# Forgetting attention in a two-layer trunk: layer 1's projections run four steps ahead, its keys move as 80 partitions, and the row of maxima is made by transposes

## The chip, the cores and the metric

The kernel runs on one core of one Trainium2 chip. The metric is the time of the program on the device in microseconds (us), as the median of several runs.

## The reference, cut to what matters

One sequence of 2048 rows of 1024 channels goes through two layers. Layer 0 is a gated recurrence beside a pooling mixer; the change does not touch it. Layer 1 is attention with a forget bias, 16 heads of 64 channels:

```python
def odd_mixer(h, w_in, b_f, qnorm_g, knorm_g, w_out):
    proj = (h @ w_in).astype(jnp.float32)
    q, k, v, g, fl = jnp.split(proj, [FOX_WIDTH, 2 * FOX_WIDTH, 3 * FOX_WIDTH, 4 * FOX_WIDTH], axis=-1)
...
    q = rms_norm(hd(q), qnorm_g).transpose(0, 2, 1, 3)
    k = rms_norm(hd(k), knorm_g).transpose(0, 2, 1, 3)
...
    logf = jax.nn.log_sigmoid(fl + b_f.astype(jnp.float32))
    cumf = jnp.cumsum(logf, axis=1).transpose(0, 2, 1)
...
        logits = (jnp.einsum('bhqd,bhkd->bhqk', q[:, :, q0:q1], k[:, :, :q1]) * scale
                  + cumf[:, :, q0:q1, None] - cumf[:, :, None, :q1])
        mask = jnp.arange(q0, q1)[:, None] >= jnp.arange(q1)[None, :]
        probs = jax.nn.softmax(jnp.where(mask, logits, -jnp.inf), axis=-1)
        outs.append(jnp.einsum('bhqk,bhkd->bhqd', probs, v[:, :, :q1]))
    o = jnp.concatenate(outs, axis=2).transpose(0, 2, 1, 3).reshape(b_, s_, FOX_WIDTH)
    o = o * jax.nn.silu(g)
    return o.astype(h.dtype) @ w_out
```

The term of the query's own `cumf` cancels in the softmax, so that the kernel adds to each logit only the key's bias and takes away the query's maximum.

## The kernel before, in words

**Segments.** The 2048 rows are taken as four segments of 512 (`s` = 0 to 3). For each, layer 0 runs and then layer 1; the output projection of layer 1 of a segment is woven into layer 0 of the next. Float32 numbers are split in a high and a low part (`split_lo`, L182), and a projection makes three matmul passes over the parts: one step of it (`proj_N`, or one step of a gate) is 8 x 3 matmuls of 128x256 (or 128x512 for the gates) on TensorE.

**Keys and queries of a head.** `prep(s, h)` (L1057) makes four transposes `pqkT` out of the normalised projection `qk`, and from them `Q1`, `K1` (128 partitions: high and low parts) and `Q3`, `K2` (68 partitions: 64 channels and 4 rows of constants and biases). The rows 64 to 67 of `K2` come by a transfer from `cfd` (high and low part of the key's bias, 1, 1; L1078), those of `Q3` from `q4d` (1, 1, 0, 0; L1077). `K1` and `K2` are also stored in DRAM, as `k1d` and `k2d`, for the later segments, which load them again as `K1o` (128 x 512) and `K2o` (68 x 512; `old_k2`, three buffers).

**Maximum.** `max_pass(s, h)` multiplies `Q3` by all keys (`pmx`), reduces each product along the keys on VectorE (L1100, L1102) to `m` (L1107: 128 queries x 4 blocks), makes `-m` and its low part (`mh` L1110, `mhl` L1111 and L1112), transposes `mhl` in one matmul (`pmt`), copies it to `mr` (L1117), and a transfer on ScalarE's queue (L1118) writes the rows 66 and 67 of `Q3`.

**Attention of a head.** `attend(s, h)` goes over blocks of 128 keys: `pst` is `K1` by `Q1` plus `K2` by `Q3` (68 rows: key channels, the bias, minus the maximum), plus a mask `mk` in the diagonal blocks. ScalarE takes the exponential twice (`ph` L1157, `pst` L1158), VectorE makes the low part `pl` (L182), GpSimd adds the sum `la`, and TensorE multiplies by the values (`pov`, `pol`). At the end, ScalarE copies a half of the result (`u`, L1179) and splits `la` (`lh`, L1184). The first product with `Q3` of a head is the first instruction that needs its maxima.

**Order.** `quad_attention` interleaves `attend` of head h with `max_pass` of head h+1; at the end of head h it runs `prep(h+2)`. Into this, `weave` puts the steps of `fill` on TensorE, evenly: `quad_fill(s, j)` is the queries and keys of two pairs of heads (`qk_pair`, 4 steps each), the gates of a quad of heads (4 steps) and the values of the next quad (`v_quad`, 4 steps), 16 steps in all, 8 for the last quad. Before each quad of heads, `fill` is made anew, and it is drained at its end; `need` drains it up to the pair that `prep` reads. `fill` of quad 0 is there from before head 0, and `keep=16` keeps all 16 steps of it for the quad. The last quad's fill also takes the first steps of the next segment (`pre0`). A scheduler then sets each engine's queue, by program order as a priority; an engine takes its instructions in order. Weights are loaded on SyncE's queue (`raw`, L288), cast on ScalarE (`wt`, L293), and their low part is made by VectorE or GpSimd (L182).

**Normalisation.** `qk_pair` copies each product (L1015), squares it (L1017), sums (L1018), takes a reciprocal root on 16 numbers a row (`rsqrt_mean`, L164 to L172) and multiplies (L1022) before the pair's first transposes.

All matmuls stand in the profile under L40 and all transposes under L43, the lines of the two helpers; in the changed file those are L42 and L45.

Of the kernel before, what the change touches and what calls it, by code (L numbers as in the profile page):

```python
# [27 lines left out]
VW = 2 * HD + 2  # L28
EPS = 1e-6
# [4 lines left out]
def trunk(ctx, tc, x, cvec, norm_g, ada_c, ada_w, ada_b, ada_bg, lbp, w0, w0o, w1, w1f, w1o,  # L34
# [118 lines left out]
    k2d = dr.tile([NH, HD + 4, T], F32, name="k2d")  # L153
    vd = dr.tile([NH, P, T // P, VW], F32, name="vd")
    cfd = dr.tile([NH, 4, T], F32, name="cfd")
    q4d = dr.tile([4, SEG], F32, name="q4d")
# [819 lines left out]
    def forget_rows(s, act):  # L976
# [22 lines left out]
        nc.sync.dma_start(cfd[:, 0, s * SEG:(s + 1) * SEG], f(ch_))  # L999
        nc.sync.dma_start(cfd[:, 1, s * SEG:(s + 1) * SEG], f(cl))  # L1000
# [56 lines left out]
    def prep(s, h):  # L1057
# [19 lines left out]
        nc.scalar.dma_start(f(Q3[HD:HD + 4]), q4d)  # L1077
        nc.scalar.dma_start(f(K2[HD:HD + 4]), cfd[h, :, s * SEG:(s + 1) * SEG])  # L1078
        if s < NSEG - 1:
            nc.sync.dma_start(k1d[h, :, s * SEG:(s + 1) * SEG], f(K1))  # L1080
            nc.sync.dma_start(k2d[h, :, s * SEG:(s + 1) * SEG], f(K2[0:HD + 4]))
        L["ops", h] = (Q1, Q3, K1, K2)

    def old_k2(h, c):
        K2 = kp.tile([P, SEG], F32R, name="K2o", tag="k2o", bufs=3)
        nc.sync.dma_start(f(K2[0:HD + 4]), k2d[h, :, c * SEG:(c + 1) * SEG])
        return K2

    def max_pass(s, h):
# [30 lines left out]
    def attend(s, h):  # L1120
# [18 lines left out]
        for c in range(s + 1):  # L1139
# [8 lines left out]
            for b in range(NTB):  # L1148
# [4 lines left out]
                mm(st[:, q0:], k2[0:HD + 4, ks], Q3[0:HD + 4, q0:], start=False, stop=(c < s))  # L1153
# [54 lines left out]
    LAG = 2  # L1208

# [23 lines left out]
    def layer1(s, xs):  # L1233
# [155 lines left out]
```

## Time and profile before

| | us |
|---|---|
| median of 3 runs | 3073.19 (3065.78 to 3075.12) |
| the profiled execution | 3059.16 |
| its span in the profile | 3057.4 |
| TensorE busy | 2799.8 (92%) |
| VectorE busy | 2373.8 (78%) |
| ScalarE busy | 1792.8 (59%) |
| GpSimd busy | 1191.7 (39%) |

The span goes from the first to the last instruction. Busy times of the engines overlap. PE is TensorE, DVE VectorE, ACT ScalarE, POOL GpSimd and SP SyncE; names of tiles stand without buffer numbers, so `Q<-mr` is the transfer of L1118 (`Q` is Q3), `K` and `Q` stand for K1, K2, Q1, Q3. [...]

### The profile page before, as it was taken

To read this page: it belongs to the slowest core of one execution; us is meant where nothing else is said; L and a number is where in the kernel's file an instruction comes from. 1 tells how busy PE (TensorE), PEld (TensorE's weight loads), DVE (VectorE), ACT (ScalarE), POOL (GpSimd) and SP (SyncE) were. 2 spreads that over 40 slices of the span, in tenths; PEclk is the share of its full clock that TensorE was granted. 3 is DMA by queue.
4 is the path that set the end of the run, shared out by engine and by line. 5 is a ranking of instruction groups with operands and counts; after the bars stand their busy time and mean duration, and the time that the engine had idled before them with its cause. 6 is when DMAs were issued, how large, how long until landed. Compare 5 with 4: busy or idle time off the path is not lost.

```text
span 3057.4 us, 49147 instructions
## 1 busy us (share of the span) xinstructions
PE 2799.8 (92%) x17020; PEld 2378.7 (78%) x17020; DVE 2373.8 (78%) x4646; ACT 1792.8 (59%) x3679; POOL 1191.7 (39%) x992
## 2 busy tenths in 40 slices
PE   4999898999998898999999899989999999999998
PEld 4888877879887777779888677777888977676767
DVE  8877688867676888876677888888758688888886
ACT  3454566763545666674445666667544566666674
POOL 3321233323212444434111555554421246655565
PEclk9999999999999999999999999999999999999999
DMA  6423454424234334434234343443333323333342
GB/s 247 163 78 104 120 141 106 122 77 128 73 114 111 101 96 109 130 90 135 68 102 118 111 108 115 117 125 106 115 99 94 110 90 101 103 96 99 92 135 79
DMA packets 198904, 338.56 MB, mean 111 GB/s; under 512 B 19768, under 2 KB 67000, under 8 KB 196096
## 3 DMA queue, kind: packets, MB, share of 16 engines
q1 hardware_dynamic: 195264, 321.52, 36.3%
q10 hardware_dynamic: 3392, 13.90, 1.3%
q8 instruction: 135, 2.21, 0.3%
q14 instruction: 113, 0.93, 0.1%
HBM read 285.72 MB, written 49.36 MB: 110 GB/s over the span
## 4 chain that ended last, share of the span: by engine, by line
PE 49%; DVE 16%; DMA 6%; ACT 5%; issue 3%; POOL 0%; SPq 0%; DVEq 0%; ACTq 0%; POOLq 0%
PE py L40 9%; PE pst L40 6%; PE pgt L40 6%; PE pqk L40 6%; PE pv L40 4%; PE pmx L40 3%; DMA K2o<-k2d 3%; PE pov L40 3%; PE pol L40 2%; PE pq L40 2%; DVE pl L182 2%; PE pl L40 2%; PE pf L40 2%; DVE wt L182 2%; DMA Q<-mr 2%
## 5 line engine op out<-in xcount | busy, mean ns | idle before, releaser
L182 POOL TENSOR_TENSOR wt<-raw,wt 128x512 fp32r<-128x512 f32 x287 | 431.3, 1511 | 998.1 <-ACT wt L293 931.9
L1168 POOL TENSOR_TENSOR la<-la,ph 128x512 f32<-128x512 f32 (+3 forms) x528 | 614.6, 1164 | 445.4 <-ACT ph L1157 396.5
L1157 ACT ACTIVATE ph<-pst 128x512 fp32r<-128x512 f32 (+3 forms) x640 | 341.6, 534 | 277.6 <-PE pst L40 258.6
L182 DVE TENSOR_TENSOR pl<-pst,ph 128x512 fp32r<-128x512 f32 (+3 forms) x640 | 385.7, 604 | 123.2 <-ACT pst L1158 111.1
L40 PE MATMUL pqk<-wt,h 128*128 128x256 f32 x3072 | 457.4, 286 | 5.7 <-DVE h L495 2.6
L40 PEld LDWEIGHTS pqk<-wt,h 128*128 128x128 f32 x3072 | 426.4, 192 | 29.8 <-DVE h L495 3.4
L40 PE MATMUL pgt<-h,wt 128*128 128x512 f32 x1536 | 418.5, 406 | 0.2 <-ACT e L527 0.2
L293 ACT CAST wt<-raw 128x512 fp32r<-128x512 f32 x578 | 337.3, 622 | 72.2 <-PE py L40 33.3
L40 PE MATMUL pv<-wt,h 128*128 128x256 f32 x2304 | 346.9, 295 | 6.0 <-DVE h L182 4.3
L40 PEld LDWEIGHTS pv<-wt,h 128*128 128x128 f32 x2304 | 324.1, 200 | 22.7 <-DVE h L182 6.4
L1158 ACT ACTIVATE pst<-pst 128x512 f32<-128x512 f32 (+3 forms) x640 | 340.1, 531 | 0.0
L40 PEld LDWEIGHTS pgt<-h,wt 128*128 128x128 f32 x1536 | 290.4, 194 | 62.0 <-issue 1.9
L182 DVE TENSOR_TENSOR wt<-raw,wt 128x512 fp32r<-128x512 f32 x291 | 264.2, 912 | 54.7 <-ACT wt L293 53.2
L1100 DVE TENSOR_REDUCE mxs<-pmx 128x1 f32<-128x512 f32 x384 | 258.4, 685 | 46.9 <-PE pmx L40 43.4
L40 PE MATMUL py<-wt,o 128*128 128x256 f32 x1536 | 203.6, 287 | 1.3 <-ACT o L1204 1.2
L40 PE MATMUL py<-wt,mix 128*128 128x256 f32 x1536 | 198.4, 287 | 3.0 <-DVE yt L842 2.1
L40 PEld LDWEIGHTS py<-wt,o 128*128 128x128 f32 x1536 | 194.2, 193 | 7.0 <-ACT o L1204 1.5
L40 PEld LDWEIGHTS py<-wt,mix 128*128 128x128 f32 x1536 | 187.7, 191 | 10.7 <-issue 4.5
L40 PE MATMUL pst<-Q,K2o 68*128 68x512 f32 x384 | 150.2, 412 | 39.6 <-DMA Q<-mr 23.0
L40 PE MATMUL pst<-Q,K1o 128*128 128x512 f32 x384 | 161.9, 427 | 18.8 <-DVE pl L182 18.2
L40 PE MATMUL pov<-ph,Vo 128*128 128x512 f32 x384 | 164.5, 428 | 4.4 <-ACT ph L1157 2.9
L40 PE MATMUL pst<-Q,K 128*128 128x512 f32 (+7 forms) x512 | 131.8, 335 | 37.1 <-DVE pl L182 27.9
(254 smaller groups left out, 5307.4 us busy)
## 6 DMA issues: line engine op xcount, KB each, us to landing
raw<-in_w_dram SPq DMA_DIRECT2D x448, 256.0 KB
K2o<-k2d SPq DMA_DIRECT2D x192, 136.0 KB
Vo<-vd SPq DMA_DIRECT2D x96, 260.0 KB
K1o<-k1d SPq DMA_DIRECT2D x96, 256.0 KB
raw<-in_w1o_dram SPq DMA_DIRECT2D x66, 256.0 KB
raw<-in_w0o_dram SPq DMA_DIRECT2D x64, 256.0 KB
vd<-Vc SPq DMA_DIRECT2D x48, 260.0 KB
ada<-in_ada_w_dram ACTq DMA_DIRECT2D x12, 1024.0 KB
```

The source lines that it names most:

```text
L40: return nc.tensor.matmul(*a, **k)
L182: (eng or V).tensor_tensor(out_t, full, f(hi), op=ALU.subtract)
L293: S.copy(wt[:, 0, sl, :], raw)
L1100: V.tensor_reduce(mxs[:, i, c:c + 1], pm[:, 0:n], axis=AX.X, op=ALU.max)
L1157: S.activation(ph[:, q0:], st[:, q0:], AF.Exp)
L1158: S.activation(st[:, q0:], st[:, q0:], AF.Exp)
L1168: G.tensor_tensor(la[:, q0:], la[:, q0:], f(ph[:, q0:]), op=ALU.add)
```

## The change

**The row of maxima.** `mh`, `mhl`, `mr` and the transfer of L1118 are gone. Each of the four columns of `m` is transposed by itself into a piece of one row `pt[0:1]` in PSUM, four transposes in place of one, and one ScalarE instruction (L1114 in the changed file) writes `-m` rounded to one fp32r number into row 64 of `Q3`. The exact value doesn't matter, as the same number divides out. Row 64 of the keys is 1, rows 65 and 66 are the bias, and the products read 67 rows (`KR`).

**Keys as 80 partitions.** `k2d`, `cfd` and `q4d` get rows up to `KX` = 80 and 16; the rows 67 to 79 are zeros that nothing reads. All transfers of `K2`, `K2o` and the constant rows move 80 or 16 partitions instead of 68 or 4. Instead of four stores of ones, `cfd` gets four of ones and four of 13 rows of zeros (`constants`).

**Steps ahead.** `fill` lives through the whole segment. Before quad 0, the weave of `max_pass(s, 0)` keeps 12 steps instead of 16, so that 4 run there; each quad adds the fill of the next quad and keeps all but 4 of the steps that it added. In quad 2 the first two steps of `pre0` come ahead of the fill of quad 3, and quad 3 adds the rest of `pre0` (in the last segment, `out_most`).

```diff
+KR = HD + 3
+KX = HD + 16
...
-    k2d = dr.tile([NH, HD + 4, T], F32, name="k2d")
+    k2d = dr.tile([NH, KX, T], F32, name="k2d")
-    cfd = dr.tile([NH, 4, T], F32, name="cfd")
-    q4d = dr.tile([4, SEG], F32, name="q4d")
+    cfd = dr.tile([NH, 16, T], F32, name="cfd")
+    q4d = dr.tile([16, SEG], F32, name="q4d")
...
-        nc.scalar.dma_start(f(Q3[HD:HD + 4]), q4d)
-        nc.scalar.dma_start(f(K2[HD:HD + 4]), cfd[h, :, s * SEG:(s + 1) * SEG])
+        nc.scalar.dma_start(f(Q3[HD:KX]), q4d)
+        nc.scalar.dma_start(f(K2[HD:KX]), cfd[h, :, s * SEG:(s + 1) * SEG])
...
-        nc.sync.dma_start(f(K2[0:HD + 4]), k2d[h, :, c * SEG:(c + 1) * SEG])
+        nc.sync.dma_start(f(K2[0:KX]), k2d[h, :, c * SEG:(c + 1) * SEG])
...
-        mhl = small([P, 2, NTB], "mhl")
-        mh = small([P, NTB], "mh", F32R)
-        V.tensor_scalar(mh, m, -1.0, None, op0=ALU.mult)
-        V.tensor_copy(mhl[:, 0, :], f(mh))
-        V.scalar_tensor_tensor(mhl[:, 1, :], m, -1.0, f(mh), op0=ALU.mult, op1=ALU.subtract)
         yield
         pt = ps_misc("pmt")
-        transpose(pt[0:2 * NTB, 0:P], mhl.rearrange("p a b -> p (a b)"))
-        mr = sp.tile([2 * NTB, P], F32R, name="mr", tag="mr", bufs=1)
-        V.tensor_copy(mr, pt[0:2 * NTB, 0:P])
-        nc.scalar.dma_start(f(Q3[HD + 2:HD + 4].rearrange("a (b t) -> a b t", t=P)), f(mr))
+        for i in range(NTB):
+            transpose(pt[0:1, i * P:(i + 1) * P], m[:, i:i + 1])
+        S.activation(Q3[HD:HD + 1], pt[0:1], AF.Copy, scale=-1.0)
...
-        weave(max_pass(s, 0), NTB * (s + 1) + 1, fill, keep=16)
+        weave(max_pass(s, 0), NTB * (s + 1) + 1, fill, keep=16 - AHEAD)
         L["mix"] = big.tile([P, ND, 2, SEG], F32R, name="o1", tag="act")
+        more = s + 1 < NSEG
         for quad in range(4):
-            if quad:
-                fill = Steps()
-            more = quad == 3 and s + 1 < NSEG
-            if more:
+            before = fill.n
+            if quad == 2 and more:
                 pre = pre0(s + 1)
                 fill.add(take(pre, 2), 2)
-            n = 16 if quad < 3 else 8
-            if s == 0 and quad == 1:
-                fill.add(both(quad_fill(s, quad), ada_gate1()), n + 9)
-            elif quad:
-                fill.add(quad_fill(s, quad), n)
-            if more:
+            if s == 0 and quad == 0:
+                fill.add(both(quad_fill(s, 1), ada_gate1()), 16 + 9)
+            elif quad < 3:
+                fill.add(quad_fill(s, quad + 1), 16 if quad < 2 else 8)
+            elif more:
                 fill.add(pre, NPRE - 2)
-            elif quad == 3:
+            else:
                 fill.add(out_most(s, L), 14)
-            weave(quad_attention(s, quad, fill), 16 * (s + 1), fill, keep=2 if more else 0)
+            ahead = AHEAD if more or quad < 2 else 0
+            keep = fill.n - before - ahead if quad < 3 else 2 if more else 0
+            weave(quad_attention(s, quad, fill), 16 * (s + 1), fill, keep=keep)
```

What it moves on the engines is seen at three places. The first is TensorE's queue at the end of the fourth head of segment 1, where the row for the next head is made (`pmt`), its keys and those of the one after are transposed (`pqkT`), and the next head's first scores (`pst` with K1o, then with K2o) follow. Before:

```order
L40 MATMUL pov_11036<-ph_11228,Vc_9930 128x128
L40 MATMUL pqk_11336<-wt_10964,h1_9623 128x256 x3
L43 MATMUL pmt_11248<-ident_85,mhl_11183 8x128
L43 MATMUL pqkT_11253<-ident_85,qk_10692 128x128
L40 MATMUL pol_11037<-pl_11231,Vc_9930 66x128
L43 MATMUL pqkT_11253<-ident_85,qk_10692 128x128 x3
L40 MATMUL pqk_11336<-wt_10964,h1_9623 128x256 x21
L40 MATMUL pst_11361<-Q1_11015,K1o_11289 128x512
L40 MATMUL pqk_11336<-wt_10964,h1_9623 128x256 x8
L40 MATMUL pmx_11283<-K2o_11281,Q3_11259 128x512
L40 MATMUL pst_11295<-Q3_11016,K2o_11291 128x512
```

And in the changed kernel:

```order
L45 MATMUL pmt_11293<-ident_85,m_11231 1x128 x4
L45 MATMUL pqkT_11299<-ident_85,qk_10475 128x128
L42 MATMUL pov_11034<-ph_11273,Vc_9867 128x128
L45 MATMUL pqkT_11299<-ident_85,qk_10475 128x128 x2
L42 MATMUL pol_11035<-pl_11276,Vc_9867 66x128
L45 MATMUL pqkT_11299<-ident_85,qk_10475 128x128
L42 MATMUL pst_11333<-Q1_11013,K1o_11327 128x512
L42 MATMUL pst_11333<-Q3_11014,K2o_11329 128x512
```

The 32 projection matmuls (`pqk`) that stood between the transposes of the maxima and the first product with `Q3` now stand elsewhere; ten matmuls remain between.

The second place is ScalarE's queue at the same head's end: the last exponentials of the head, the copies `u` and `lh`, and how the maxima get into `Q3`. Before:

```order
L1157 ACTIVATE ph_11228<-pst_11224 128x128
L1158 ACTIVATE pst_11224<-pst_11224 128x128
L1077 DMA Q3_11259<-q4d_175 4x512
L1179 COPY u_10935<-pov_11036 64x512
L1078 DMA K2_11261<-cfd_174 4x512
L1184 CAST lh_11244<-la_11035 128x512
L1118 DMA Q3_11016<-mr_11250 2x4x128
L1071 ACTIVATE Q1_11258<-pqkT_11253,c_qkg_513 64x512
```

And in the changed kernel, where the new instruction L1114 stands ahead of `u` at this head and behind it at the next one (the last three rows):

```order
L1079 DMA Q3_11305<-q4d_175 16x512
L1153 ACTIVATE ph_11273<-pst_11269 128x128
L1154 ACTIVATE pst_11269<-pst_11269 128x128
L1114 ACTIVATE Q3_11014<-pmt_11293 1x512
L1175 COPY u_10993<-pov_11034 64x512
L1073 ACTIVATE Q1_11304<-pqkT_11299,c_qkg_513 64x512
...
L1175 COPY u_11552<-pov_11325 64x512
L1114 ACTIVATE Q3_11305<-pmt_11561 1x512
L1073 ACTIVATE Q1_11572<-pqkT_11567,c_qkg_513 64x512
```

The transfer that stood behind `lh` became an instruction on the engine; `u` (or, at six heads of segment 0, `lh`) stands ahead of it at 38 of the 64 heads.

The third place is TensorE's queue at the head before, where the first transposes of a new pair stand. `qk_10692` (before) and `qk_10475` (changed) are the same pair's normalised projection. Before:

```order
L40 MATMUL pol_11037<-pl_11073,Vo_11042 66x512
L40 MATMUL pv1_11141<-wt_10675,h1_9623 128x256 x5
L43 MATMUL pqkT_11010<-ident_85,qk_10692 128x128 x4
L40 MATMUL pv1_11141<-wt_10675,h1_9623 128x256 x18
L40 MATMUL pmx_11032<-K2o_11030,Q3_11016 128x512
```

And in the changed kernel:

```order
L45 MATMUL pmt_11002<-ident_85,m_10939 1x128 x3
L45 MATMUL pqkT_11008<-ident_85,qk_10475 128x128 x2
L42 MATMUL pol_10723<-pl_10984,Vc_9867 66x128
L45 MATMUL pqkT_11008<-ident_85,qk_10475 128x128 x2
L42 MATMUL pst_11042<-Q1_10701,K1o_11036 128x512
L42 MATMUL pqk_11080<-wt_10767,h1_9560 128x256 x3
L42 MATMUL pst_11042<-Q3_10702,K2o_11038 128x512
```

The pair's last projection row stands 37 rows ahead of these transposes before and 76 rows ahead in the changed kernel. The first pair of each segment isn't moved: its projection stands 3 rows ahead in both.

## Rows read from the trace of the kernel before

**Rows 1.** The page's part 1: busy us, share, instructions.

```profile
PE 2799.8 (92%) x17020; PEld 2378.7 (78%) x17020; DVE 2373.8 (78%) x4646; ACT 1792.8 (59%) x3679; POOL 1191.7 (39%) x992
```

**Rows 2.** Windows, segment 3's attention: from:to, us, each engine's busy us, PEclk, DMA share, GB/s.

```profile
2438.00:3057.00 619.00, 566.86 (x3112) 453.05 (x3111) 516.62 (x939) 403.36 (x796) 350.58 (x287) 0.97 0.33 101
```

**Rows 3.** Waits of TensorE over the span: total us, times, longest us.

```profile
PE pst L40 <- DVE pl L182: 46.1, 61, 3.4
PE pqkT L43 <- DVE qk L1022: 31.2, 27, 2.9
PE pst L40 <- DMA Q<-mr: 30.9, 14, 6.3
PE pmt L43 <- DVE mhl L1112: 19.0, 20, 1.7
PE pst L40 <- DMA K2o<-k2d: 16.4, 19, 2.0
```

**Rows 4.** Timeline of PE from 1061.5: start us, us, instruction, [idle before <-releaser].

```profile
1063.52 0.33 PE L40 MATMUL pov<-ph,Vc 128*128 128x128 f32 x1 [0.17 <-ACT ph L1157]
...
1065.06 2.76 PE L40 MATMUL pqk<-wt,h 128*128 128x256 f32 x21
...
1070.54 0.73 PE L40 MATMUL pst<-Q,K2o 68*128 68x512 f32 x2 [1.30 <-DMA Q<-mr]
```

**Rows 5.** The same stretch on ACT.

```profile
1063.37 0.27 ACT L1158 ACTIVATE pst<-pst 128x128 f32<-128x128 f32 x1
1063.88 0.58 ACT L1179 COPY u<-pov 64x512 f32<-64x512 f32 x1 [0.25 <-PE pov L40]
...
1065.82 0.62 ACT L1184 CAST lh<-la 128x512 fp32r<-128x512 f32 x1 [1.35 <-DVE la L1180]
1065.82 0.62 ACTq L1118 DMA_DIRECT2D Q<-mr  x1
```

**Rows 6.** The same stretch on DVE.

```profile
1061.90 0.15 DVE L1107 TENSOR_REDUCE m<-mxs 128x4 f32<-128x8 f32 x1
...
1064.79 0.28 DVE L1117 CAST mr<-pmt 8x128 fp32r<-8x128 f32 x1 [0.17 <-PE pmt L43]
```

**Rows 7.** Groups by line: busy us, mean ns of one | idle before.

```profile
L293 ACT CAST wt<-raw 128x512 fp32r<-128x512 f32 x578 | 337.3, 622 | 72.2 <-PE py L40 33.3 <-issue 9.1 <-DMA raw<-in_w_dram 8.5
...
L1110 DVE TENSOR_SCALAR mh<-m 128x4 fp32r<-128x4 f32 x64 | 25.5, 398 | 0.9
...
L1111 DVE COPY mhl<-mh 128x4 f32<-128x4 f32 x64 | 22.6, 353 | 1.1
...
L1112 DVE SCALAR_TENSOR_TENSOR mhl<-m,mh 128x4 f32<-128x4 f32 x64 | 13.3, 208 | 0.0
```

**Rows 8.** Timeline of PE, first head of segment 0.

```profile
368.19 0.79 PE L40 MATMUL pst<-Q,K 68*128 68x512 f32 x1 [4.78 <-DMA Q<-mr]
```

**Rows 9.** Windows after such a wait and at a head's end in segment 3.

```profile
365.40:372.20 6.80, 4.01 (x16) 3.40 (x17) 1.25 (x2) 1.87 (x4) 1.61 (x2) 0.50 0.81 220
2570.40:2573.80 3.40, 3.40 (x18) 3.30 (x17) 2.31 (x4) 1.80 (x3) 0.16 (x1) 0.50 0.39 148
```

**Rows 10.** Timeline of DVE and PE, head's end in segment 3.

```profile
2564.91 0.16 DVE L1107 TENSOR_REDUCE m<-mxs 128x4 f32<-128x16 f32 x1
...
2569.36 0.27 PE L43 MATMUL pmt<-ident,mhl 128*8 128x128 f32 x1 [1.53 <-DVE mhl L1112]
```

**Rows 11.** Timeline of PE and DVE, a pair's last projection to its first transposes.

```profile
1035.78 1.84 PE L40 MATMUL pqk<-wt,h 128*128 128x256 f32 x14
...
1050.08 2.31 DVE L1022 TENSOR_TENSOR qk<-qk,ssq 128x1024 f32<-128x1024 f32 x1
...
1052.45 0.66 PE L43 MATMUL pqkT<-ident,qk 128*128 128x128 f32 x4 [1.59 <-DVE qk L1022]
```

**Rows 12.** The page's part 6: transfers, count, KB each.

```profile
K2o<-k2d SPq DMA_DIRECT2D x192, 136.0 KB
...
K1o<-k1d SPq DMA_DIRECT2D x96, 256.0 KB
```

More of the change, by code (lines that the diff above doesn't have):

```diff
@@ L998, in forget_rows @@
         split_lo(cl, cf, ch_)
-        nc.sync.dma_start(cfd[:, 0, s * SEG:(s + 1) * SEG], f(ch_))
-        nc.sync.dma_start(cfd[:, 1, s * SEG:(s + 1) * SEG], f(cl))
+        nc.sync.dma_start(cfd[:, 1, s * SEG:(s + 1) * SEG], f(ch_))
+        nc.sync.dma_start(cfd[:, 2, s * SEG:(s + 1) * SEG], f(cl))
     seg1 = [dict() for _ in range(NSEG)]
@@ L1076, in prep @@
         S.copy(K2[lo], f(K1[up]))
-        nc.scalar.dma_start(f(Q3[HD:HD + 4]), q4d)
-        nc.scalar.dma_start(f(K2[HD:HD + 4]), cfd[h, :, s * SEG:(s + 1) * SEG])
+        nc.scalar.dma_start(f(Q3[HD:KX]), q4d)
+        nc.scalar.dma_start(f(K2[HD:KX]), cfd[h, :, s * SEG:(s + 1) * SEG])
         if s < NSEG - 1:
             nc.sync.dma_start(k1d[h, :, s * SEG:(s + 1) * SEG], f(K1))
-            nc.sync.dma_start(k2d[h, :, s * SEG:(s + 1) * SEG], f(K2[0:HD + 4]))
+            nc.sync.dma_start(k2d[h, :, s * SEG:(s + 1) * SEG], f(K2[0:KX]))
         L["ops", h] = (Q1, Q3, K1, K2)
@@ L1097, in max_pass @@
                 pm = ps_mx("pmx")
-                mm(pm[:, 0:n], Q3[0:HD + 4, i * P:(i + 1) * P], kc[0:HD + 4, 0:n], start=True, stop=True)
+                mm(pm[:, 0:n], Q3[0:KR, i * P:(i + 1) * P], kc[0:KR, 0:n], start=True, stop=True)
                 if c < s:
@@ L1152, in attend @@
                 mm(st[:, q0:], k1[:, ks], Q1[:, q0:], start=True, stop=False)
-                mm(st[:, q0:], k2[0:HD + 4, ks], Q3[0:HD + 4, q0:], start=False, stop=(c < s))
+                mm(st[:, q0:], k2[0:KR, ks], Q3[0:KR, q0:], start=False, stop=(c < s))
                 if c == s:
@@ L1208, in trunk @@
     LAG = 2
+    AHEAD = 4
     def quad_attention(s, quad, fill):
@@ L1300, in constants @@
         V.memset(z1, 0.0)
-        nc.sync.dma_start(q4d[0:2, :], o1[0:2])
-        nc.sync.dma_start(q4d[2:4, :], z1[0:2])
+        nc.sync.dma_start(q4d[1:3, :], o1[0:2])
+        nc.sync.dma_start(q4d[0:1, :], z1[0:1])
+        nc.sync.dma_start(q4d[3:16, :], z1[0:13])
         for s in range(NSEG):
-            nc.sync.dma_start(cfd[:, 2, s * SEG:(s + 1) * SEG], o1[0:NH])
-            nc.sync.dma_start(cfd[:, 3, s * SEG:(s + 1) * SEG], o1[0:NH])
+            nc.sync.dma_start(cfd[:, 0, s * SEG:(s + 1) * SEG], o1[0:NH])
+            nc.sync.dma_start(cfd[:, 3:, s * SEG:(s + 1) * SEG], z1[0:NH].unsqueeze(1).to_broadcast([NH, 13, SEG]))
         wfr = tmp("wfr", F32, (P, ND, NH))
```

## The prediction, made before the changed kernel ran

> **What bounds the kernel now.** I read the page's busy times first [rows 1]: TensorE works 2799.8 of 3057.4 us, so the whole prize for removing waits is the 258 us in which it stands still, and any new matmul is paid in full. VectorE follows at 78%; in segment 3's attention it is busy 516.62 of 619 us, 83% [rows 2], so there it can become the bound. Then the waits of TensorE by what ended them [rows 3]. Five rows matter. Four belong to what the change touches: first transposes of a pair waiting for the normalisation (31.2 us), first scores of a head waiting for the transfer of the maxima (30.9), the maxima's transpose waiting for `mhl` (19.0), and scores waiting for `K2o` (16.4). Together 97.5 us. The fifth, scores waiting for `pl` on VectorE (46.1), is not touched directly. The chain that ended last gives the `K2o` loads 3% of the span, which is much more than TensorE ever waits for them; I go by the waits. Last the timelines of a head's end [rows 4 to 6], to see how long the chain from the maximum to the row takes and what covers it.
>
> **How the numbers relate.** Durations come from the profiled execution, 3059.16 us. It lies 14.0 us (0.46%) under the median of the three runs shown, 3073.19. The sum is made against 3059.2, and the result is then raised by 0.46%.
>
> **Part 1, the row of maxima.**
>
> (a) The transfer goes, and with it its wait: -30.9 us over 14 waits [rows 3]. The largest are at the first head of segments; the one of segment 0 is 4.78 us [rows 8]. [...] At these first heads I leave 1 us each of wait for the new chain (3 us). Sum: -34.
>
> (b) `pmt` no longer waits for three small VectorE instructions (398 + 353 + 208 ns of their own, [rows 7]), which stand in a queue between larger ones: in segment 3 `m` ended at 2565.07, and its transpose ran at 2569.36, 1.53 us of that idle [rows 10]. A wait for `m` itself stays possible, so I take -17 of the 19.0 [rows 3]. After five such waits in segment 3 the clock stood at 0.50 for 3.4 us with about 3.3 us of work [rows 9], half of which comes back: -8. Sum: -25.
>
> (c) New work on TensorE: four transposes for one, 192 more. Four transposes take 0.66 us and one 0.27 ([rows 11], [rows 10]), so each further one (0.66 - 0.27)/3 = 0.13 us: +25, on the path.
>
> (d) The new wait. The row is now a ScalarE instruction of one partition and 512 elements out of PSUM; the trace has none such. The nearest is `u`, 64 x 512 out of PSUM, 0.58 us [rows 5]; below, a 128 x 128 one takes 0.27 [rows 5]. I take 0.58, since the number of elements in a row is the same. Before, the transfer had 29 projection matmuls as cover (21 of them took 2.76 us, 0.12 each, [rows 4]) and at this head even so 1.30 us too little. In the changed order they are gone from there. At this head, `pov` starts at 1063.52 [rows 4]; then come in the new order three transposes (0.39), a small product (0.12) and one 512-column product (twice a 256-column one, 0.23), so TensorE reaches the first product with `Q3` at 1063.52 + 0.12 + 0.74 = 1064.38. If `u` stands first on ScalarE, it ends at 1064.46 [rows 5] and the row at 1065.04: a wait of 0.7. If the row stands first, it starts when the last exponential ends, 1063.64 [rows 5], and is done at 1064.22: no wait. In the new order `u` (or `lh`) is first at 38 heads: +27. On TensorE all that stands behind that product waits with it. Behind the row on ScalarE, while it waits for the transposes, stand `u` and the copies of `prep`, which nobody needs within a microsecond. Bounds: 0 if ScalarE is always free, and for 64 heads 0.7 + 0.62 (a weight cast in front too, [rows 7]) = 1.3, or 83.
>
> (e) VectorE loses 25.5 + 22.6 + 13.3 us [rows 7] and 64 copies `mr` of 0.28 [rows 6], 79 us. That could shorten the 46.1 us of waits for `pl`; at a head's end it should, but I take 0 and keep 20 for the range. ScalarE gains 64 x 0.58 us and loses 64 issues of 0.62 [rows 5]: even.
>
> **Part 2, four steps ahead.** (f) In one timeline a pair's last projection ran to 1037.6, the normalisation ended at 1052.39, and the transposes waited 1.59 us for it [rows 11]. In the new order the distance in front of the transposes doubles (76 rows of TensorE's queue for 37). The 27 waits of at most 2.9 us [rows 3] should go, but not at the first pair of each segment, which isn't moved; four of them at 2 us (between the mean, 31.2/27 = 1.2, and the longest) stay: -23. The four steps themselves (about 4 x 24 x 0.12 = 11.5 us) are only moved into the time before head 0, where the waits of (a) lay. Their weight loads go with them on SyncE's queue, ahead of the loads of old keys and values, and their casts on ScalarE and low parts on VectorE or GpSimd; queue positions move, the amount doesn't: 0, and where that pushes `K2o` back, its term below is lost (12).
>
> **Part 3, 80 partitions.** (g) `K2o` moves 160 KB for 136, and 18% more bytes could make it later. But the K1o load beside it moves 256 KB over 128 partitions [rows 12], and no wait of TensorE [rows 3] names it. So the shape and not the size seems to be what delays `K2o`; I take -12 of the 16.4 us, with the bounds 0 and -16.4. [...] The other transfers (constant rows, stores, 13 rows of zeros at the start) have no waiting reader: 0.
>
> **Sum:** -34 - 25 + 25 + 27 - 23 - 12 = -42 us, 3017 against 3059.2; raised by 0.46%, **3031**. A change of 0.3% (9 us) is about what a measurement can tell.
>
> **The rivals.**
>
> *Stronger.* ScalarE is mostly free when `pmt` ends, so the new waits come to 10 us (-17), and the relief of VectorE takes 20 off `pl`: -79, 2980, on the median **2994**. For it: ScalarE is busy 59% only [rows 1], and `u` waited for TensorE at this head [rows 5]. Against: `u` does stand first at 38 heads. Chance 0.14.
>
> *Slower.* ScalarE's queue is the new transfer. A weight cast of 0.62 us stands with `u` in front of the row at nearly every head, so that 64 heads wait 1.3 us: 83 instead of 27 (+56). A wait of 1.53 us at this place in segment 3 was followed by the 0.50 clock ([rows 10], [rows 9]), so the 14 us of (a) and (b) for it are not given back either: -42 + 56 + 14 = +28, on the median **3101**. It decides from a mean wait of (42 + 27)/64 = 1.1 us on. For it: 578 such casts are spread over the run [rows 7], and at the head of the timelines the issue of the transfer, ready when `mr` ended at 1065.07, went out at 1065.82 only, with `lh`, which had waited 1.35 us for `la` ([rows 5], [rows 6]). Against: at most heads the exponentials directly precede the row. [...] Chance 0.12.
>
> *No change.* The waits come back one instruction later, as waits for `pl`: VectorE is at 83% in segment 3 [rows 2], and TensorE that arrives earlier only stands before it. If 40 of the 97.5 us return, the sum is -2 and the median **3071**. For it: 46.1 us already go there [rows 3]. Against: 79 us of VectorE's work go, too. Chance 0.14.
>
> *That the change doesn't do what it says*, the scheduler putting the steps back, is out: its order shows them ahead. Only the `K2o` term could be empty (+12, in the range).
>
> **How the numbers follow.** The forecast has 0.60. Its own spread, from the bounds of (d), (e) and (g), is about 3000 to 3070. Faster by over 0.3%: nearly all of the forecast (0.55) and the stronger case, 0.69. Within: 0.04 of the forecast and most of the case of no change, 0.14. Slower: the slower case, 0.01 of the forecast, 0.02 of no change, and 0.02 for the measurement, 0.17. The range, 2990 to 3082, leaves out the slower case, and what lies beyond the stronger one.
>
> **What would show it.** In the profile after: no `Q<-mr`, and in its place a wait of `pst` for `Q` on ScalarE of about 27 us in some 38 pieces (over 70: the slower case); of the waits of `pqkT` for `qk` four left, about 8 us; `pmt` waiting for `m` under 3 us; waits for `K2o` under 5; the stretches at clock 0.50 at first heads and at head ends of segment 3 gone; TensorE busy longer by some 11 us (25 of transposes less 14 of clock), VectorE shorter by 79. The prediction is wrong if the waits for `pl` rise by more than 20 us, or if those for the row pass 70.

## The result and the profile after

| | before | changed |
|---|---|---|
| median of 4 runs, first set | 3069.49 us (3058.59 to 3075.12) | 3031.65 us (3025.02 to 3035.85) |
| ratio, first set | | 0.9889 (95%: 0.9868 to 0.991) |
| median, a later set | 3047.56 us (7 runs) | 3028.85 us (4 runs) |
| ratio, later set | | 0.9935 (95%: 0.9915 to 0.9954) |
| the profiled execution | 3059.16 us | 3029.48 us |

The change makes the kernel faster by 0.65 to 1.1%. The kernel before moves between sets (medians of 3069.5, 3054.0, 3051.4 and 3047.6 us in the four), the changed one hardly, so below an experiment is compared with the kernels of its own set first, by ratio.

The page's busy times of the changed kernel, to stand beside [rows 1]:

```profile
PE 2808.9 (93%) x17212; PEld 2390.2 (79%) x17212; DVE 2301.3 (76%) x4390; ACT 1826.4 (60%) x3743; POOL 1172.5 (39%) x992
```

TensorE is busy 9.1 us longer (the prediction said 11) and VectorE 72.5 us less (said 79). The span fell by 29.6 us, so TensorE stands still some 39 us less. Where it still waits (total us, times, longest us), to stand beside [rows 3]:

```profile
PE pst L42 <- DVE pl L184: 35.1, 31, 2.4
PE pd L42 <- DVE kT L535: 22.4, 1, 22.4
...
PE pmx L42 <- ACT Q L1077: 10.2, 19, 1.5
PE pqkT L45 <- DVE qk L1024: 9.6, 6, 2.5
...
PE pst L42 <- ACT Q L1114: 6.4, 9, 1.8
...
PE pmt L45 <- DVE m L1109: 1.5, 2, 1.1
...
PE pst L42 <- DMA K2o<-k2d: 1.2, 2, 1.0
```

Of the five rows of before, four are as good as gone: 97.5 us came down to 9.6 + 6.4 + 1.5 + 1.2 = 18.7. The wait for `pl` fell by 11. But a wait of 22.4 us stands there that the kernel before doesn't have, once, for layer 0's `kT`; and one of 10.2 for the copy of `Q3` in `prep`. The groups of the new work:

```profile
L45 PE MATMUL pmt<-ident,m 128*1 128x128 f32 x256 | 42.2, 272 | 2.6 <-DVE m L1109 1.5 <-DVE xt L489 1.1
...
L1114 ACT ACTIVATE Q<-pmt 1x512 fp32r<-1x512 f32 x64 | 37.4, 585 | 11.1 <-PE pmt L45 9.8
```

The transposes `pmt` cost 42.2 us; in the kernel before, the group of `pmt` is busy 17.7 us in 64 pieces. That is +24.5 (predicted 25), and the row takes 585 ns (predicted 0.58).

Where did the time go? Windows of the kernel before, from the first projection of layer 1 to the end of the last scores, segments 0 and 3 (from:to, us, busy us of PE, PEld, DVE, ACT, POOL, PEclk, DMA share, GB/s; PEclk is the granted clock of TensorE as a share of its full one):

```profile
316.20:673.10 356.90, 320.38 (x2098) 278.56 (x2097) 278.61 (x596) 231.64 (x496) 111.29 (x108) 0.98 0.42 114
...
2422.70:3036.70 614.00, 564.59 (x3096) 450.70 (x3093) 519.00 (x939) 413.41 (x827) 350.23 (x284) 0.97 0.33 100
```

And of the changed kernel:

```profile
342.90:697.30 354.40, 327.77 (x2158) 285.95 (x2157) 268.58 (x534) 243.09 (x517) 110.56 (x109) 0.98 0.47 119
...
2419.80:3006.70 586.90, 556.79 (x3144) 446.67 (x3143) 491.13 (x875) 421.39 (x844) 352.42 (x284) 0.99 0.38 110
```

Segment 0 of layer 1 gained 2.5 us and segment 3 gained 27.1. But the first projection comes at 342.9 us where it came at 316.2: **the changed kernel loses 26.7 us before layer 1 starts at all.** From there to the end it gains some 56. SyncE's queue shows why. Before, the weight loads that stand behind the stores of the constants (start us, us, instruction):

```profile
53.34 10.10 SPq L288 DMA_DIRECT2D raw<-in_w_dram  x4
```

In the changed kernel, the first of the four stores of 13 rows of zeros (`cfd<-z`), and the same weight loads:

```profile
49.26 0.32 SPq L1304 DMA_DIRECT2D cfd<-z  x1
...
86.31 8.32 SPq L290 DMA_DIRECT2D raw<-in_w_dram  x4
```

The four weight loads go out at 86.31 instead of 53.34. What SyncE's queue waited for between 40 and 110 us (total, times, longest):

```profile
SPq L1304 <- DMA ada<-in_ada_w_dram: 15.8, 3, 7.7
...
SPq L1303 <- DMA ada<-in_ada_w_dram: 12.8, 1, 12.8
```

By the profile the stores (L1303, L1304) stood there behind loads of `ada`, which another queue issues, and the weights stood behind the stores. Their number isn't new: the kernel before has eight stores of ones at these places (not four, as the text on the change says), of 32 KB each, where the changed one has four such stores of ones and four of zeros, those of 416 KB each. The wait on TensorE that came of it:

```profile
104.28 0.80 PE L42 MATMUL pd<-qT,kT 128*128 128x128 f32 x2 [22.40 <-DVE kT L535]
```

### The profile page after: what moved, and what is told of

Its sections match the earlier page's. It is cut to its first block, busy times and chain, and to the rows that moved or that the text cites. A ratio compares the mean times of both kernels' runs of the same rounds, so it can differ in the third digit from the quotient of the medians.

```text
span 3027.8 us, 49244 instructions
## 1 busy us (share of the span) xinstructions
PE 2808.9 (93%) x17212; PEld 2390.2 (79%) x17212; DVE 2301.3 (76%) x4390; ACT 1826.4 (60%) x3743; POOL 1172.5 (39%) x992
## 4 chain that ended last, share of the span: by engine, by line
PE 60%; DVE 19%; ACT 11%; DMA 4%; issue 4%; POOL 1%; SPq 0%; ACTq 0%; DVEq 0%; POOLq 0%
PE py L42 10%; PE pgt L42 8%; PE pqk L42 8%; PE pst L42 6%; PE pv L42 6%; PE pmx L42 4%; PE pov L42 3%; PE pol L42 3%; PE pf L42 3%; PE pq L42 3%; PE pl L42 3%; DVE pl L184 2%; DVE wt L184 2%; ACT wt L295 1%; DMA raw<-in_w_dram 1%
## 5 line engine op out<-in xcount | busy, mean ns | idle before, releaser
L184 POOL TENSOR_TENSOR wt<-raw,wt 128x512 fp32r<-128x512 f32 x287 | 419.5, 1470 | 1030.9 <-ACT wt L295 975.1
L1164 POOL TENSOR_TENSOR la<-la,ph 128x512 f32<-128x512 f32 (+3 forms) x528 | 610.6, 1156 | 385.7 <-ACT ph L1153 342.9
L42 PE MATMUL pqk<-wt,h 128*128 128x256 f32 x3072 | 433.1, 286 | 5.5 <-DVE h L497 2.7
L42 PEld LDWEIGHTS pqk<-wt,h 128*128 128x128 f32 x3072 | 411.9, 192 | 25.2 <-DVE h L497 3.5
L42 PE MATMUL pgt<-h,wt 128*128 128x512 f32 x1536 | 403.9, 405 | 0.0
L1102 DVE TENSOR_REDUCE mxs<-pmx 128x1 f32<-128x512 f32 x384 | 258.6, 684 | 20.3 <-PE pmx L42 17.2
L42 PE MATMUL pmx<-K2o,Q 67*128 67x512 f32 x384 | 162.0, 426 | 21.9 <-ACT Q L1077 10.2
L1104 DVE CUSTOM_DVE_ANT_0 pmx<-pmx,mq 128x128 f32<-128x128 f32 (+3 forms) x256 | 124.6, 497 | 55.6 <-PE pmx L42 53.8
```

Source lines behind the costliest of these rows:

```text
L42: return nc.tensor.matmul(*a, **k)
L184: (eng or V).tensor_tensor(out_t, full, f(hi), op=ALU.subtract)
L1102: V.tensor_reduce(mxs[:, i, c:c + 1], pm[:, 0:n], axis=AX.X, op=ALU.max)
L1104: V.tensor_tensor_reduce(pm[:, 0:n], pm[:, 0:n], mq[:, SEG - n:], 1.0, NEG, op0=ALU.add, op1=ALU.max, accum_out=mxs[:, i, c:c + 1])
L1164: G.tensor_tensor(la[:, q0:], la[:, q0:], f(ph[:, q0:]), op=ALU.add)
```

## The experiments

Three theories were to be told apart. The *sum of the prediction*: each part is worth what its waits add up to, and the stores at the start cost nothing. The *start-up theory*, read from the profile above: the stores cost about 25 us, and the parts are worth more than forecast. And the *interplay theory*: the parts cover for each other, so that one alone is worth little or less than nothing.

**Zeros late.** The 13 rows of zeros of a segment are stored at the start of that segment's layer 1.

```diff
         act = L["act"] = big.tile([P, ND, 2, SEG], F32R, name="h1", tag="act")
+        z1 = tmp("z1")[0:NH]
+        G.memset(z1, 0.0)
+        nc.sync.dma_start(cfd[:, 3:, s * SEG:(s + 1) * SEG], z1.unsqueeze(1).to_broadcast([NH, 13, SEG]))
...
-            nc.sync.dma_start(cfd[:, 3:, s * SEG:(s + 1) * SEG], z1[0:NH].unsqueeze(1).to_broadcast([NH, 13, SEG]))
```

> The changed kernel, but the 13 rows of zeros of cfd are stored segment by segment at the start of that segment's layer 1 instead of all at the start of the program. Theory A (the prediction's: those stores have no waiting reader and cost nothing): as the changed kernel, 3031 us, within 5. Theory B (they keep SyncE's queue from the first weight loads, so that TensorE starts layer 0 late: the first projection of layer 1 comes at 342.9 us instead of 316.2): about 25 us less, 3003 to 3010, and the 22.4-us wait of pd for kT is gone.

Measured: 2993.73 us, 0.9799 of before (0.9779 to 0.9819), for 0.9889 of the change. Theory B holds for the start, and the gain is larger than it said. The weight loads go out early again:

```profile
51.80 1.80 SPq L290 DMA_DIRECT2D raw<-in_w_dram  x4
```

The first projection of layer 1 comes at 316.5 us, and the wait for `kT` is gone. Against the changed kernel that is 27 us by the ratios, 38 by the medians and 34 in the profiled executions. 26.4 us of the last are the start. One other wait fell as well, that of `pqkT` for `qk`, from 9.6 us to the first row here (total, times, longest):

```profile
PE pqkT L45 <- DVE qk L1024: 2.1, 6, 0.8
...
PE pst L42 <- DMA K2o<-k2d: 2.0, 3, 1.0
```

That this came with the moved store wasn't expected, and its cause is open. It isn't what the remaining 7.6 us are made of: from the first projection of layer 1 on, TensorE's idle time is the same in both (146.8 us and 147.7), as other waits rose, and its busy time is 8.5 us less (2538.2 and 2529.7). A second profile of the unaltered changed kernel has 2534.5 there, so part of the 8.5 is spread. This run beats both kernels, and the next ones start from it.

**Zeros on another queue.** The stores stay at the start, as in the change, but are issued on GpSimd's queue.

```diff
-            nc.sync.dma_start(cfd[:, 3:, s * SEG:(s + 1) * SEG], z1[0:NH].unsqueeze(1).to_broadcast([NH, 13, SEG]))
+            nc.gpsimd.dma_start(cfd[:, 3:, s * SEG:(s + 1) * SEG], z1[0:NH].unsqueeze(1).to_broadcast([NH, 13, SEG]))
```

> The changed kernel with the 13 rows of zeros stored at the start as in the change, but issued on GpSimd's queue. Theory A (it is SyncE's queue: the stores stand ahead of the weight loads there and wait for older transfers): the first weight loads behind the constants are issued at some 53 us as before, and the time is within 6 us of the run with late zeros, 0.980 of before. Theory B (it is the 1.7 MB themselves that take the bandwidth from the weights): the loads go out early but land late, and the time is nearer to the changed kernel, 0.986 to 0.990 of before.

Measured: 3003.07 us, 0.9837 (0.9809 to 0.9866), 9 us above the run with late zeros, where theory A allowed 6, and below the band of theory B. SyncE's queue shows that the loads wait less, but not as little as before:

```profile
47.63 0.38 SPq L290 DMA_DIRECT2D raw<-in_w_dram  x1
61.09 10.60 SPq L290 DMA_DIRECT2D raw<-in_w_dram  x7
```

One load goes at 47.63 and the others at 61.09. Yet the first projection of layer 1 stands at 315.2 us: the whole start is won back with the same bytes stored at the start of the program. It was the queue. What is left above the run with late zeros lies behind the start, 11.2 us in the profiles, and is mostly busy time: TensorE works 8.0 us longer there and stands still 3.2 us longer, though its wait for `qk` is 8.8 us again.

**68 partitions.** From the changed kernel, with `KX` = `HD + 4`; `cfd`, `q4d` and their stores shrink with it, so that four stores of one row of zeros (32 KB each) stand at the start where the change has 13 rows.

```diff
-KX = HD + 16
+KX = HD + 4
```

> The changed kernel with 68 instead of 80 partitions for the keys (4 rows of constants, one row of zeros). Both theories take the start-up cost from the run with late zeros. Theory A (the shape made K2o late): waits of pst for K2o return to about 16 us, 12 to 16 us above the run with late zeros. Theory B (the new order of the loads covers K2o whatever its shape): waits under 4 us and the same time as the run with late zeros, within 5.

Measured: 3021.34 us, 0.9889 (0.9868 to 0.991), 28 us above the run with late zeros (22 in the profiled executions). The start is as in the kernel before, with the first projection of layer 1 at 313.9 us, though the stores of zeros stand on SyncE's queue as in the change; the weight loads behind them:

```profile
54.07 10.06 SPq L290 DMA_DIRECT2D raw<-in_w_dram  x4
```

So the price of the start takes both, that queue and large stores. Why the stores wait there when large ones are among them (15.8 and 12.8 us above) and hardly when all are small (5.2 us in the kernel before) isn't shown. The waits of TensorE:

```profile
PE pst L42 <- DMA K2o<-k2d: 17.8, 17, 3.0
```

17.8 us for `K2o` in 17 waits, where the run with late zeros has 2.0 in 3: theory A by the waits. Only 187 of TensorE's 17,212 places in the order differ between the two, so it is the shape. The time is about twice what theory A allowed; 20.3 us of it are seen in the windows of the attention of segments 2 and 3, with 68 partitions:

```profile
1636.80:2151.00 514.20, 476.98 (x2647) 383.93 (x2648) 412.98 (x747) 360.52 (x728) 260.28 (x216) 0.97 0.40 113
2421.00:2994.70 573.70, 539.60 (x2985) 428.42 (x2986) 472.03 (x841) 403.66 (x796) 343.59 (x278) 0.99 0.33 102
```

and in the run with late zeros:

```profile
1637.30:2139.80 502.50, 467.64 (x2647) 377.03 (x2648) 414.27 (x748) 360.78 (x729) 263.54 (x217) 0.99 0.46 122
2408.00:2973.10 565.10, 536.66 (x2986) 428.33 (x2986) 474.30 (x842) 403.74 (x797) 346.12 (x280) 0.99 0.38 110
```

11.7 and 8.6 us, 20.3 together. In segment 2 it is mostly not idle time: the same 2647 matmuls were busy 476.98 us instead of 467.64, with a clock of 0.97 instead of 0.99. This slower clock didn't follow the waits for `K2o`: of six there (6.9 us), one, of 2.9 us, has a stretch at 0.50 behind it. Five waits for `pl` of 1.6 to 1.8 us at heads' ends stand in both runs; with 68 partitions four of them go with such a stretch, with late zeros two. One of the other three, and the window that starts where the wait ends, with the clock at 1.00:

```profile
1848.02 0.50 PE L42 MATMUL pst<-Q,K1o 128*128 128x512 f32 x1 [1.83 <-DVE pl L184]
...
1848.00:1851.40 3.40, 2.75 (x12) 1.77 (x12) 3.40 (x5) 1.22 (x3) 2.38 (x2) 1.00 0.26 93
```

**The same wait, 1.6 to 1.8 us, cost its own time alone at some heads, and a stretch at clock 0.50 as well at others.** What decides between the two isn't shown.

**The old row.** From the run with late zeros: the three VectorE instructions, the one transpose, the copy and the transfer of before, in rows 66 and 67 of 80 (`KR` is 68, and the rows of the bias and of ones stand where they stood before).

```diff
-        for i in range(NTB):
-            transpose(pt[0:1, i * P:(i + 1) * P], m[:, i:i + 1])
-        S.activation(Q3[HD:HD + 1], pt[0:1], AF.Copy, scale=-1.0)
+        transpose(pt[0:2 * NTB, 0:P], mhl.rearrange("p a b -> p (a b)"))
+        mr = sp.tile([2 * NTB, P], F32R, name="mr", tag="mr", bufs=1)
+        V.tensor_copy(mr, pt[0:2 * NTB, 0:P])
+        nc.scalar.dma_start(f(Q3[HD + 2:HD + 4].rearrange("a (b t) -> a b t", t=P)), f(mr))
```

> The run with late zeros, but the row of maxima is made the old way (three VectorE instructions, one transpose, a copy and the transfer into two rows). Theory A (the prediction's sum for part 1: -34 -25 +25 +27): 7 us above the run with late zeros. Theory B (with the projections run ahead nothing covers the transfer any more, which takes some 3 us from the transpose to the row): about 1 to 2 us more of wait at each of 64 heads, 60 to 120 us above the run with late zeros.

Measured: 3033.77 us, 0.9927 (0.9907 to 0.9948), 40 us above. Both theories miss, A by far (7), B less (60 to 120). B's 3 us are there in the kernel before: from the start of the transpose `pmt` to the end of the transfer's last packet its trace has a median of 2.9 us over the 64 heads. The waits:

```profile
PE pst L42 <- DMA Q<-mr: 29.4, 15, 5.2
...
PE pmx L42 <- DVE mxs L1102: 14.9, 23, 1.9
...
PE pmt L45 <- DVE mhl L1114: 12.0, 12, 1.9
...
PE pst L42 <- DMA K2o<-k2d: 4.3, 5, 1.8
```

29.4 us for the transfer, 12.0 for `mhl`, and 14.9 of the maxima's products for VectorE. The 24.5 us of the additional transposes are saved here, so the old row costs more than the 40 us in the rest.

**No steps ahead.** From the run with late zeros, `AHEAD = 0`.

```diff
-    AHEAD = 4
+    AHEAD = 0
```

> The run with late zeros with AHEAD = 0: each quad's weave uses up its own steps, none of the next quad's. Theory A (the prediction's part 2: the wait of pqkT for qk returns): 23 us above the run with late zeros, with that wait at about 30 us. Theory B (the order of the steps also decides whether projections cover the waits at a head's start): more than 35 us above, with waits of pst for the row too. Theory C (steps ahead do nothing, the new row does all): within 5 us.

Measured: 3019.88 us, 0.9882 (0.9858 to 0.9906), 26 us above: theory A by its time. The waits:

```profile
PE pqkT L45 <- DVE qk L1024: 19.9, 26, 2.1
...
PE pst L42 <- DMA K2o<-k2d: 15.6, 9, 4.6
```

That for `qk` is at 19.9 and not 30, and 15.6 for `K2o` are new, though those loads have 80 partitions.

**Each part alone, on the kernel before.** First the row of maxima (67 rows read, 68 moved, the old order of steps); its edit is that of `max_pass` in the change.

> The kernel before with the new row of maxima alone (68 partitions, the old order of the steps). The prediction's sum for this part: -7 us, with new waits for the row of 27 us. Theory B, from the run with the old row (which lost 40 us against the one with late zeros): most of it is gained alone, -20 to -30 us. Theory C (without the other two, other waits take its place): within 5 us of before, while those for K2o or for qk grow.

Measured: 3037.32 us, 0.9966 (0.9951 to 0.9981), -10 us by the ratio: the prediction's sum for the part, not theory B. Waits:

```profile
PE pqkT L45 <- DVE qk L1024: 25.9, 21, 2.6
PE pst L42 <- DMA K2o<-k2d: 24.6, 19, 5.8
```

The waits for the row are 2.5 us and not 27, so more should have come; `K2o`, 16.4 us before, takes 24.6, and `pov` waits 16.4 us for the exponentials, where before it waited 5.6. TensorE stands before the next late thing.

Then the steps ahead alone; its edit is that of `layer1` in the change.

> The kernel before with the steps run four ahead alone. The prediction's sum: -23 us, the wait of pqkT for qk down from 31 to about 8. Theory B (the projections that now run earlier were the cover of the transfer of the maxima): that wait goes, but those for the transfer grow by as much, so that the time is within 8 us of before.

Measured: 3064.54 us, 1.0039 (1.0021 to 1.0056): **slower by 12 us**. Waits:

```profile
PE pst L40 <- DMA Q<-mr: 33.1, 15, 5.6
PE pst L40 <- DVE pl L182: 27.9, 49, 1.5
PE pst L40 <- DMA K2o<-k2d: 19.6, 19, 2.5
PE pmx L40 <- DVE mxs L1100: 13.7, 21, 1.9
...
PE pqkT L43 <- DVE qk L1022: 7.7, 5, 2.2
```

The wait for `qk` fell from 31.2 to 7.7, just as forecast, and nothing was gained. This isn't quite theory B: the waits for the transfer of the maxima grew by 2.2 us only (33.1 for 30.9), those for `K2o` by 3.2, those for the reductions to 13.7 from 2.3; but those for `pl` fell from 46.1 to 27.9, and as a whole TensorE stands still 12.9 us less (244.7 for 257.6). What took the gain is busy time, 2812.6 us for 2799.8 with the same instructions in another order, at a mean clock of 0.972 for 0.975. The two profiled executions take the same time (3059.0 and 3059.2 us), as that of the kernel before is from the slower first set; by the runs of one set the clocks lie further apart, 0.967 to 0.973 here and 0.973 to 0.978 before. Why the clock falls with the steps ahead isn't shown.

Then the 80 partitions alone, with the zeros stored late.

```diff
+KX = HD + 16
...
-        nc.sync.dma_start(f(K2[0:HD + 4]), k2d[h, :, c * SEG:(c + 1) * SEG])
+        nc.sync.dma_start(f(K2[0:KX]), k2d[h, :, c * SEG:(c + 1) * SEG])
```

> The kernel before with 80 partitions alone, the zeros stored late. The prediction's sum: -12 us, with the waits for K2o (16 us) down to 2 to 4. Theory B, from the run with 68 partitions (28 us above the one with late zeros, only 18 of them waits, the rest a lower clock after them): -15 to -28 us. Theory C (alone the gain is taken by the next wait, for pl or for the transfer of the maxima): within 5 us.

Measured: 3015.56 us, 0.988 (0.9856 to 0.9905), -37 us: more than any theory gave. Waits:

```profile
PE pst L42 <- DMA Q<-mr: 19.1, 12, 4.8
PE pmt L45 <- DVE mhl L1114: 14.8, 19, 1.7
...
PE pst L42 <- DMA K2o<-k2d: 1.9, 3, 0.7
```

`K2o` went from 16.4 to 1.9, as forecast. On top of it, TensorE is busy 2781.6 us for 2799.8 with 17020 instructions in both, 18 us, at a mean clock of 0.982 for 0.975. The waits for the transfer of the maxima fell as well, from 30.9 to 19.1. What `K2o` has to do with those wasn't tried, and the order isn't the same: 1631 of TensorE's 17,020 places differ, so this pair alone doesn't price the shape. A cleaner pair is on record: the run with the old row is the one with the steps ahead alone plus the 80 partitions and nothing else, and 22 places differ. There `K2o` goes from 19.6 us to 4.3, and the time from 1.0039 to 0.9927, 34 us (24 in the profiled executions).

**The parts in pairs.** The three alone sum to -10 + 12 - 37 = -35 us; together, in the run with late zeros, they give -61. The runs above hold every pair of the parts as well, and so say where the other 26 us come from (us by the ratio to the kernel before of the same set, of some 3050; each is good to about 6 us):

| parts in the kernel | run | us |
|---|---|---|
| row | the row alone | -10 |
| ahead | the steps alone | +12 |
| 80 | the partitions alone | -37 |
| row, ahead | 68 partitions | -34 |
| row, 80 | no steps ahead | -36 |
| ahead, 80 | the old row | -22 |
| all three | late zeros | -61 |

The 80 partitions are worth 26 to 37 us beside any of the others. The row and the steps ahead need each other: the row is worth 10 us or nothing without the steps, and 46 or 39 with them; the steps cost 12 to 14 us without the row, and gain 24 to 25 with it. (The run with no steps ahead keeps the new way of filling the quads, so that its order isn't quite the old one.) That projections had been the cover of the old row's chain fits this, but as an account of the time it is argued: the waits for `mr` and `mhl` together fell from 49.9 to 45.6 us when the steps came alone, and rose from 33.9 to 41.4 beside the 80 partitions.

**The row twice.** From the run with late zeros, the ScalarE instruction of the row is issued two times.

```diff
         S.activation(Q3[HD:HD + 1], pt[0:1], AF.Copy, scale=-1.0)
+        S.activation(Q3[HD:HD + 1], pt[0:1], AF.Copy, scale=-1.0)
```

> The run with late zeros, but ScalarE writes the row of maxima twice, 0.58 us more between the transposes and the row at each of 64 heads. Theory A (the prediction's term d: the row is on the path at 38 heads): 22 us or more above the run with late zeros (38 x 0.58), and waits of pst for the row of over 25 us. Theory B (the row is done when TensorE gets there, as its small waits say): under 10 us above.

Measured: 3021.27 us, 0.991 (0.9889 to 0.993), 28 us above by the medians, 34 by ratio. The time is theory A's, but not the waits:

```profile
PE pst L42 <- ACT Q L1115: 15.2, 29, 1.0
...
PE pst L42 <- DMA K2o<-k2d: 13.3, 6, 2.9
```

15.2 us for the row, and the `K2o` waits are back. The scheduler also laid TensorE's queue differently, in 2720 of 17,212 places, so this isn't a clean price: inconclusive, beyond that the row isn't far from the path.

**The changed kernel again**, beside these on one chip, unaltered.

> The changed kernel unaltered, beside the others on one chip. Both theories: 0.989 of before, and 25 to 28 us above the run with late zeros.

Measured: 3028.85 us, 0.9935 (0.9915 to 0.9954). The time is that of the first set within 3 us; the ratio is not, since the kernel before took 3047.56 here. The next run, on the same chip, with the zeros stored late and one copy moved, is 31 us below, which agrees with the price of the start.

**Q3's copy first.** From the run with late zeros, in `prep`:

```diff
         S.activation(Q1[lo], pt[lo], AF.Copy, scale=g[lo])
+        S.copy(Q3[lo], f(Q1[lo]))
         S.activation(K1[up], pt[up], AF.Copy, scale=g[up])
...
-        S.copy(Q3[lo], f(Q1[lo]))
```

> The run with late zeros with the copy of Q3 (ScalarE) moved ahead of K1's in prep, so that the wait of pmx for that copy (10.3 us in 20 pieces) goes. Theory A (that wait is on the path): 5 to 10 us below the run with late zeros. Theory B (the next wait takes its place): within 5 us.

Measured: 2997.56 us, 0.9829 (0.9809 to 0.985): nothing gained, theory B. The wait is still there, for the next instruction of `prep`'s chain:

```profile
PE pmx L42 <- ACT Q L1074: 9.6, 17, 1.5
```

**Eight steps ahead.** `AHEAD = 8`, from the run with late zeros.

> The run with late zeros with 8 steps ahead instead of 4. Theory A (what steps ahead bring is cover for the normalisation of a pair, and four steps give all of it): within 6 us of the run with late zeros. Theory B (every step that is moved out of the heads leaves them with less to hide behind): 10 us or more above, with more waits for pl and for the row.

Measured: 3021.13 us, 0.9909 (0.9878 to 0.9941), 27 us above: theory B. Waits for `K2o` are back, 11.1 us in 7 pieces, and for the reductions, 9.5 us in 22; those for `pl` fell (33.4 us for 36.4) and those for the row rose by 3.1 us only, so theory B is right by its time and not by its waits. That fewer projections are left in the heads to stand before these waits is the likely reason, and not shown.

## Why the prediction was right, and where it was not

The time, 3031.65 us for 3031, is right, and faster was the likeliest; but that it is right to a microsecond is luck. Two errors work against each other: layer 1 gained more than forecast (about 56 us in the profile for 42), and the start took 27 back. What is left of them, 29.7 us for the 42 of the sum, is a miss of 12 us in the profiled executions (3029.5 us for 3017), and a third error hides it: the sum was raised by 0.46%, 14 us, because the median of the kernel before lay that far above its profiled execution, and the median of the changed kernel lies only 2.2 us above its own.

- **(a), (b) the waits for the transfer and for `mhl`**: gone, as forecast (30.9 and 19.0 to 0 and 1.5). Of the -34 of (a), 6 us stood for the clock at first heads, and no run shows that term by itself. What the trace of before shows is three stretches of 6.8 us at clock 0.50, with 3.6 to 4.7 us of TensorE work in each (a product of 512 columns took 0.79 us in the first of them, [rows 8], and 0.39 at clock 1.00); one is left in the changed kernel (segment 2, 3.4 us), and the five at head ends of segment 3 went. Others came: one of 23.9 us around the wait at the start, and five at head ends of segment 2, so that the mean clock stayed at 0.975. From the first projection of layer 1 on, the time at 0.50 fell from 135 to 109 us by the clock records of the two traces. One of the five, 3.4 us:

```profile
1994.00:1997.40 3.40, 3.40 (x12) 2.64 (x10) 3.40 (x7) 1.08 (x2) 1.76 (x2) 0.50 0.21 73
```

  All five stand at a wait for `pl` of 1.6 to 1.8 us; another of them:

```profile
1761.86 0.80 PE L42 MATMUL pst<-Q,K1o 128*128 128x512 f32 x1 [1.83 <-DVE pl L184]
```

  This is the case of no change on a small scale: TensorE arrives earlier and stands before VectorE. In the run with late zeros only two of five such waits go with the 0.50 clock, so that this part of the price isn't fixed.
- **(c) the transposes**: +24.5 for +25. Right.
- **(d) the new wait for the row**: wrong, 6.4 us in 9 waits for 27 in 38. The failed step is "TensorE reaches the first product with `Q3`" after transposes and two products: it took the order of a head where the row stands first and put `u` ahead of it. Where `u` does stand first, the scheduler had at most heads of segments 1 to 3 left projections in front of that product. Such a head of the changed kernel, on ScalarE and on TensorE:

```profile
1117.63 0.59 ACT L1175 COPY u<-pov 64x512 f32<-64x512 f32 x1
1118.24 0.59 ACT L1114 ACTIVATE Q<-pmt 1x512 fp32r<-1x512 f32 x1
...
1117.35 1.40 PE L42 MATMUL pqk<-wt,h 128*128 128x256 f32 x10
...
1118.88 0.50 PE L42 MATMUL pst<-Q,K2o 67*128 67x512 f32 x1
```

  Ten projections and a little more last until the row ends at 1118.83, and the product starts 0.05 us later, with no idle time that the timeline shows. Eight of the nine waits lie in segment 0, 0.2 to 0.8 us each (the ninth, 1.8 us, is at the first head of segment 2). There other work of ScalarE stands in front of the row as well. At one such head a weight cast does, ahead of `u`, and a single projection is the cover:

```profile
443.12 0.62 ACT L295 CAST wt<-raw 128x512 fp32r<-128x512 f32 x1
...
445.01 0.51 PE L42 MATMUL pst<-Q,K 67*128 67x512 f32 x1 [0.62 <-ACT Q L1114]
```

  So these waits have the size of the 0.7 us that was worked out, but not by `u` alone.

  Two readings were off by little: a projection takes 2.76 / 21 = 0.13 us for the 0.12 taken, and `pov` took 0.33 us in its row [rows 4] where the sum has 0.12.

  The remark that nobody needs `prep`'s copies within a microsecond was wrong as well: `pmx` waits 10.2 us for the one of `Q3`. Moving that copy gained nothing, so it was not to be had there.
- **(e) VectorE's relief**: 72.5 us less work, and 11 us less wait for `pl`; taken at 0, with 20 kept for the range.
- **(f) steps ahead**: the waits for `qk` fell to 9.6 us in 6 pieces (forecast: 8 in 4). As a count it was right, as a price it was not: alone this part costs 12 us, and with the new row it is worth 24 to 25. That the four steps "are only moved" missed that what the projections leave behind gets slower: without the new row the waits for `qk` went and the clock fell (0.972 for 0.975, and 2812.6 us of busy time for 2799.8).
- **(g) 80 partitions**: right in kind and mis-sized: -12 was taken, -37 measured alone and 26 to 34 beside the other parts. The waits went as forecast (16.4 to 1.9). Left out were the clock, which the prediction had counted in (a) and (b) and not here (0.982 for 0.975, and 18 us less of busy time), and that other waits fall too (`Q<-mr` by 11.8). That the shape and not the size delays `K2o` was read from the `K1o` loads, which no wait of TensorE names; the runs agree (19.6 us of waits with 68 partitions, 4.3 with 80, in nearly the same order), but why 68 partitions are waited for longer isn't shown, and in some orders the 80 are waited for too (15.6 us with no steps ahead).
- **"The other transfers (constant rows, stores, 13 rows of zeros at the start) have no waiting reader: 0"**: wrong by 27 us. They have no reader that waits; they have a neighbour. Behind them on SyncE's queue stood layer 0's weights. The prediction said of moved steps that queue positions move, and didn't ask of the stores what stands behind them and what their new size, 416 KB for 32, does to it.

Of the rivals, the *stronger* one was closest to what layer 1 did (row waits of 10 us there, 6.4 measured; `pl` 20 less there, 11 measured). The *slower* one's queue of ScalarE is seen, but at the heads of segment 0 and not at nearly every head.

## What to carry to other kernels

Four stores of 416 KB that nobody waits for cost 27 us here, because the weight loads stood behind them on their queue: look at the queue's next instruction, at the start above all. Moving projections forward lost 12 us by itself, and gained 24 to 25 once a chain that they stood beside had been shortened (here the row): test the parts in pairs. And look at the clock around a wait of TensorE, not at its length alone; a wait of 1.6 to 1.8 us for `pl` was followed by clock 0.50 at four of five heads in one run and at two of five in another.

## What the runs showed of the hardware that was not expected

Moving 160 KB over 80 partitions was less waited for than 136 KB over 68: 3 waits for 17 (2.0 us for 17.8) and 5 for 19 (4.3 us for 19.6) in two pairs with nearly the same instruction order, and 34 us of time in the second. Four stores of 416 KB on SyncE's queue sent the weight loads behind them out at 86.31 us instead of 53.34; four of 32 KB at the same places, at 54.07. The mean granted clock was 0.975 before, 0.982 with 80 partitions alone and 0.972 with the steps ahead alone; between those last two lie 31 us of TensorE's busy time (2781.6 and 2812.6) for the same number of instructions. It didn't follow the idle time: with the steps ahead alone TensorE stood still less than before (244.7 us for 257.6), at the lower clock.
